# One modulation vector of a decoder trunk summed by ScalarE and an adding transfer instead of VectorE

## The chip, the cores and the metric

One core of one Trainium2 chip. A core has TensorE (PE; its weight loads are listed apart as PEld), VectorE (DVE), ScalarE (ACT), GpSimd (POOL) and SyncE (SP), which run their own instruction queues in order and meet at semaphores, and 16 DMA engines that all queues share. The metric is the device time of one execution in microseconds (us), the median over runs.

## The reference

Two decoder layers on 256 tokens of width 2048, in float32. Each layer is conditioned on one vector c: from it six modulation vectors are computed per layer, each a product of c with a 2048 x 2048 block of `mod_w`.

```
c_act = silu(c)
for layer in range(2):
    mod = c_act @ mod_w[layer] + mod_b[layer]
    sh1, sc1, g1, sh2, sc2, g2 = split(mod, 6)
    h = modulate(rms_norm(x), sh1, sc1)
    y = nsa_mixer(h) if layer == 0 else sb_mixer(h, k_sh, v_sh)
    x = x + g1 * rms_norm(y)
    h = modulate(rms_norm(x), sh2, sc2)
    y = swiglu(h)               # (silu(h @ w_gate) * (h @ w_up)) @ w_out
    x = x + g2 * rms_norm(y)
```

The vector of this case is `g2` of the second layer, the gate of its second mixer (the SwiGLU). It is the last of the 14 vectors and is needed only at the end, when `x + g2 * rms_norm(y)` is formed.

## The kernel before

**Weights.** All matmuls take tiles of 512 x 512 weights, 1 MB each, loaded by SP into a page (128 x 2048 float32) called raw. ScalarE rounds a page into wh (tile type fp32r), VectorE writes the remainder wl = raw - wh, and TensorE then makes three products for each 128 x 128 block of the left side (its high and low halves with wh, its high half with wl), over two halves of the tokens: 24 matmuls of 128 x 512 per tile. The left sides are hhF (the second mixer's normed input) and fa (its activations).

**Pages.** There are 21 pages (`N_PAGES`) for everything of that size: raw, wh, wl, the left sides, modw, macc and others. A page goes from one tenant to the next; the first instruction that writes the new tenant waits, by semaphore, for the last one that used the old.

**The order.** The program is written out in advance by a planner (`Emit`, `pump`, `run`): it keeps estimated clocks of PE, ACT, DVE and the DMA queues and puts each instruction, in the order of these estimates, into its engine's queue. On the chip the order is fixed and only semaphores time it. `fill` puts small idle matmuls (128 x 256, bf16) before a matmul of TensorE where the planner expects TensorE to wait over 1.2 us. Loads are issued by SP in the order of the list `order`; for the last stage `spread` mixes the 16 pages of vector (1, 5) among its weight tiles.

**The vector.** `mac_load` makes the 16 loads of a vector. Page k, called modw, holds rows 128k to 128k + 127 of the block. VectorE forms macc = modw * cact[:, 0] for k = 0, and macc = modw * cact[:, k] + macc for the others (cact is silu(c), one value per partition); then the page is given back. 6 us of the planner's clock after the last page `mod_fin` follows: four matmuls with ones (pmod) sum macc over the partitions, a copy by ScalarE (mrow), transposes, bias and norm weight by VectorE. Later `gate_rows` writes the vector to DRAM and reads it back as the 128 x 2048 tile G, both on GpSimd's queue, which until then carries nothing in this stage. `y_block` multiplies by G.

**The stage.** The second layer's second mixer runs from about 1680 us to the end: six blocks of gate and up products (`ep_gateff` puts silu(gate) into sg, `ep_up` multiplies, transposes on TensorE, aT, and splits into fa), then a first part of the output product (into yp), five more blocks, and the rest of the output product.

Line numbers: in the profile every engine instruction stands at line 118 (119 with the change), the helper that records it; tiles are told apart by name.

Of the kernel before, what the change touches and what calls it, by code (L numbers as in the profile page):

```python
# [12 lines left out]
AF = mybir.ActivationFunctionType  # L13
OP = mybir.AluOpType
# [5 lines left out]
D = 2048  # L20
# [39 lines left out]
FILL_LEAVE = 0.7  # L60
LEADS = (5.0, 5.0, 5.0)
M_FFN = 80

C_ID, C_NTRI, C_ANY, C_NEG1, C_ONE, C_KEEP = 0, 128, 256, 258, 259, 260
C_MASK, C_MASKT, C_CMP, C_COS, C_SIN, C_END = 260, 388, 516, 548, 804, 1060
# [32 lines left out]
class Engine:  # L98
# [5 lines left out]
    def __getattr__(self, op):  # L104
        f = getattr(self.real, op)
        E, eng = self.E, self.name

        def call(*a, **k):
            acc = k.get("accum_out")
            aps = [v for v in list(a) + [v for n, v in k.items() if n != "accum_out"] if hasattr(v, "free_size")]  # L110
            out, ins = aps[0], aps[1:]
            load = 0.0
            if eng == "ACT" and a[2] in TABLES and TABLES[a[2]] != E.table:
                E.table, load = TABLES[a[2]], 1.28
            if eng == "PE":
                E.fill(aps)
            E.enter(eng, _cost(eng, op, out, ins, k, acc), [out] + ([acc] if acc is not None else []), ins, load)
            return f(*a, **k)  # L118

        return call  # L120


def _cost(eng, op, out, ins, k, acc):
    n = out.free_size()
    if eng == "PE":
        if op == "transpose":
            return 0.109
        if ins[1].dtype != F32:
            return max(n / 2400.0 + 0.0133, 0.04)
        if out.shape[0] <= 64 and n >= 128:  # L130
            return n / 2400.0 + 0.09 if out.shape[0] <= 32 else n * 2 / 2400.0 + 0.02
        return 2 * max(n * 2 / 2400.0 + 0.0133, 0.109)
    n = max([n] + [i.free_size() for i in ins])
    if eng == "ACT":
        ptr = sum(hasattr(k.get(x), "free_size") for x in ("bias", "scale")) + (acc is not None)
        return 0.08 + n * 0.000833 + 0.093 * ptr
    if eng == "DMA2":
        return 3.0
    if eng == "DMA":
        return n * 4 * P / 383e3  # L140
    fast = op in ("tensor_scalar", "tensor_copy") and out.space == ins[0].space and list(ins[0].ap)[-1][0] == 1
    ptr = 0.055 * (op in ("tensor_scalar", "scalar_tensor_tensor"))
    return 0.075 + ptr + n / (1920.0 if fast else 960.0)
# [308 lines left out]
def kernel(ctx: ExitStack, tc, consts, x, c, mod_w, mod_b, norm_g, ffn_w_in, ffn_w_out, a_w_in,  # L452
# [8 lines left out]
    E = Emit(nc)  # L461
    V, A, T, DMA = E.V, E.A, E.T, E.D
# [5 lines left out]
    def small(name, n, dt=F32):  # L468
        return cp.tile([P, n], dt, name=name)
# [74 lines left out]
    cact = small("cact", 16)  # L544
# [3 lines left out]
    def modb(vec):  # L548
        l, i = vec
        if l == 2:  # L550
            return vecT[:, 0, 96 + 16 * i:112 + 16 * i]
        return vecT[:, l, 16 * i:16 * i + 16]
# [6 lines left out]
    def mod_src(vec):  # L559
        l, i = vec  # L560
        return (mod_w[l] if l < 2 else kv_mod_w)[:, i * D:(i + 1) * D]
# [9 lines left out]
    macs = {}  # L571

    def mac_load(vec, k):
        st = {}

        def dma():
            st["t"] = E.alloc("pg", "modw")
            DMA.dma_start(st["t"], mod_src(vec)[k * P:(k + 1) * P, :])

        def mac(sl):  # L580
            if k == 0:
                if sl.start == 0:
                    macs[vec] = E.alloc("pg", "macc")
                V.tensor_scalar(macs[vec][:, sl], st["t"][:, sl], cact[:, 0:1], None, op0=OP.mult)
            else:
                V.scalar_tensor_tensor(macs[vec][:, sl], st["t"][:, sl], cact[:, k:k + 1], macs[vec][:, sl],
                                       op0=OP.mult, op1=OP.add)
            if sl.stop == D:
                E.put("pg")
                if k == 15:  # L590
                    E.spawn(after(mod_fin(vec), E.fin + (2.0 if vec[0] == 0 and vec[1] < 5 else 6.0)))

        return Load(("mod", vec, k), "mod", 1 if k == 0 else 0, dma, lambda: E.when(st["t"]),
                    lambda: mac(slice(0, D)))

    def mod_fin(vec):

        yield
        m = macs[vec]
        b = yield from E.get("x", "pmod")  # L600
        for q in range(4):
            T.matmul(b[32 * q:32 * q + 32], ones.to_broadcast([P, 32]), m[:, q * NB:(q + 1) * NB], start=True, stop=True)
        E.put("pg")
        row = yield from E.get("s2", "mrow")
        yield
        A.activation(row, b, AF.Copy)
        yield
        for j in range(4):
            T.transpose(b[:, j * P:(j + 1) * P], row[:, j * P:(j + 1) * P], ident)
        E.put("s2")  # L610
        yield
        v4 = lambda ap: ap.rearrange("p (q j) -> p q j", q=4)
        dst = v4(modT[vec])
        V.tensor_tensor(dst, b.rearrange("p (j q r) -> p q j r", j=4, q=4)[:, :, :, 0], v4(modb(vec)), op=OP.add)
        if vec in gn_of:
            g = vecT[:, 2, 16 * gn_of[vec]:16 * gn_of[vec] + 16] if vec[0] < 2 else vecT[:, 1, 96:112]
            V.scalar_tensor_tensor(dst, dst, 1.0 if vec[0] == 2 or vec[1] in sc_like else 0.0, v4(g),
                                   op0=OP.add, op1=OP.mult)
        E.put("x")
        E.flag(("mod", vec))  # L620
# [489 lines left out]
    def ep_piece(acc, t, place, p, final):  # L1110

        if p:
            yield from E.wait(("part", place, t, p - 1))
        s = yield from part_of(place, t)
        if p == KT - 1 and final[0] == "v":
            yield from ep_v(acc, t, final[1], s, lambda: part_done(place))
            return
        if p == 0:
            A.activation(s, acc, AF.Copy)
        else:  # L1120
            V.tensor_tensor(s, acc, s, op=OP.add)
        E.put("mm")
        E.flag(("part", place, t, p))
        if p == KT - 1:
            yield
            if final[0] == "q":
                yield from ep_q(s, t, final[1], lambda: part_done(place))
            else:
                yield from ep_k(s, t, "ksw", final[1], lambda: part_done(place))
# [378 lines left out]
    for kt in range(KT):  # L1508
        if kt == 0:
            first = [blk[0] for blk in whole]  # L1510
            for seg, nb, place, final in early[:0]:
                first += mm_units(seg, w0, col[seg] + nb * NB, nb, [kt], "hA",
                                  lambda a, t, nb_, place=place, final=final, kt=kt: ep_piece(a, t, place, kt, final))
# [6 lines left out]
        for seg, nb, place, final in early[0 if kt == 0 else 0:]:  # L1520
            emit_plain(mm_units(seg, w0, col[seg] + nb * NB, nb, [kt], "hA",
                                lambda a, t, nb_, place=place, final=final, kt=kt: ep_piece(a, t, place, kt, final)))
# [82 lines left out]
    def mods_of(vecs):  # L1605
        return [("mod", v, k) for v in vecs for k in range(16)]
# [3 lines left out]
    def keys_of(a, b):  # L1610
        ks = []
        for u in units[a:b]:
            k = u.get("key")
            if k and k not in seen:
                seen.add(k)
                ks.append(k)
        return ks
# [4 lines left out]
    def spread(ks, mods, tail, head=0):  # L1622


        tot = sum(cost(k) for k in ks[head:len(ks) - tail])
        o, m, c = [], 0, 0.0
        for i, k in enumerate(ks):
            if i >= head:
                c += cost(k)
            want = min(len(mods), round(len(mods) * c / tot))  # L1630
            while m < want:
                o.append(mods[m])
                m += 1
            o.append(k)
        return o
# [22 lines left out]
    m1 = mods_of([(0, 5), (2, 1), (2, 0), (1, 1), (1, 0)])  # L1658
    order += spread(keys_of(n_l0, n_f0), m1[:M_FFN], TAIL, HEAD)
    order += spread(keys_of(n_f0, n_l1), m1[M_FFN:] + mods_of([(1, 2), (1, 4), (1, 3)]), TAIL, HEAD)  # L1660
    order += spread(keys_of(n_l1, len(units)), mods_of([(1, 5)]), 20, HEAD)

    for k in order:
        if k[0] == "mod":
            E.loads.append(mac_load(k[1], k[2]))
        elif k[0] == "modq" and k[2] == "h":
            E.loads.append(macq_half(k[1], k[3], k[4]))
        elif k[0] == "modq":
            E.loads.append(macq_load(k[1], k[2], k[3]))
        elif k[0] == "w1":  # L1670
            E.loads.append(raw_load(k, a_cmp_w1[0, k[1], k[2] * 1024:(k[2] + 1) * 1024, :]))
        elif k[0] == "wg":
            E.loads.append(w_load(k, w0[:, col["g"]:col["g"] + 3 * H], 16, 3 * H))
        else:
            E.loads.append(w_load(k, wsrc[k]))
# [64 lines left out]
    def after(gen, t, calm=False):  # L1740
        yield t
        while calm and E.urgent:
            yield False
        yield from gen
# [73 lines left out]
```

## Time and profile before

| what | us |
|---|---|
| runs (2) | 2411.55 and 2412.08, median 2411.82 |
| profiled execution, first to last instruction | 2407.8 |
| PE busy | 2356.9 (98%) |
| DVE busy | 1633.4 (68%) |
| ACT busy | 1077.6 (45%) |
| all 16 sums of the vector on VectorE | from 1700.8 to 2232.9 |
| pmod of the vector | 2239.9 |
| gate written by GpSimd, then read back | 2291.7, 2295.2 |

Busy shares are averages over stages; what a change is worth is read in its stage. In a timeline a row gives start, duration, engine, line, operation, tiles and shapes, and in brackets how long the engine had been idle before it and what ended that. In a table by stretches each engine has its busy us and instruction count, then follow the granted TensorE clock (1.00 is full), the share of the DMA engines in use, and GB/s.

### The profile page before, as it was taken

Reading aid. Unit: us, or ns where it says so; the run is one execution under the profiler, and the core shown is the slowest. Engines: PE = TensorE matmul, PEld = TensorE weight load, DVE = VectorE, ACT = ScalarE, POOL = GpSimd, SP = SyncE. Lnnn points to the kernel's source line nnn. Section 1 sums busy time; section 2 is a strip of 40 time slices with the busy share of each in tenths; the row PEclk is TensorE's granted clock in tenths of the full one; section 3 lists DMA queues with packets and bytes.
Section 4 is the critical chain, followed back from the end, with each engine's and each line's share of the span. In section 5 each row is a group of like instructions: output and inputs, shape, how many; then the busy total and the mean of one; then the engine's idle time right before and its main releaser. Section 6 shows DMA issues by size and latency. Waiting matters only on the chain.

```text
span 2407.8 us, 27188 instructions
## 1 busy us (share of the span) xinstructions
PE 2356.9 (98%) x11124; PEld 1906.6 (79%) x11124; DVE 1633.4 (68%) x1346; ACT 1077.6 (45%) x1217; POOL 5.6 (0%) x14
## 2 busy tenths in 40 slices
PE   6999999999999999999999999999999999999998
PEld 4677777877888888888877788887888888888886
DVE  3788789978766667767768778865645454554554
ACT  4343455563433333333455455765433333333342
POOL 0000000000000000000000000000000000000000
PEclk9999999999999999999999999999999999999999
DMA  9998967979887699878758979845756547855642
GB/s 350 389 388 281 354 245 250 362 252 397 283 309 273 224 330 399 327 273 307 260 197 333 339 272 399 315 166 196 269 191 220 200 152 244 304 193 196 221 160 105
DMA packets 265629, 657.54 MB, mean 273 GB/s; under 512 B 12449, under 2 KB 30113, under 8 KB 240161
## 3 DMA queue, kind: packets, MB, share of 16 engines
q1 hardware_dynamic: 263808, 649.13, 75.0%
q0 software_dynamic: 992, 6.32, 0.7%
q8 instruction: 87, 1.43, 0.2%
q10 hardware_dynamic: 704, 0.36, 0.1%
q14 instruction: 38, 0.30, 0.0%
HBM read 653.64 MB, written 2.13 MB: 272 GB/s over the span
## 4 chain that ended last, share of the span: by engine, by line
PE 86%; ACT 4%; DMA 4%; DVE 3%; SPq 1%; issue 1%; ACTq 0%; DVEq 0%
PE acc L118 78%; DMA raw<-in_a_w_in_dram 2%; PE sc L118 1%; SPq L118 1%; DVE wl L118 1%; PE oT L118 1%; PE z L118 1%; ACT wh L118 1%; ACT hf L118 1%; ACT junk L118 1%; PE aT L118 1%; DMA modw<-in_mod_w_dram 1%; PE pmod L118 1%; DMA modq<-in_mod_w_dram 1%; PE hT L118 1%
## 5 line engine op out<-in xcount | busy, mean ns | idle before, releaser
L118 DVE TENSOR_TENSOR wl<-raw,wh 128x2048 fp32r<-128x2048 f32 (+2 forms) x392 | 880.0, 2249 | 516.9 <-ACT wh L118 477.8
L118 ACT ACTIVATE wh<-raw 128x2048 fp32r<-128x2048 f32 (+2 forms) x392 | 734.6, 1880 | 683.5 <-PE acc L118 478.7
L118 PE MATMUL acc<-wh,hhF 128*128 128x512 f32 x2816 | 883.7, 392 | 0.0
L118 PEld LDWEIGHTS acc<-wh,hhF 128*128 128x128 f32 x2816 | 530.4, 188 | 113.7 <-issue 4.2
L118 PE MATMUL acc<-wl,hhF 128*128 128x512 f32 x1408 | 549.3, 390 | 0.0
L118 DVE SCALAR_TENSOR_TENSOR macc<-modw,cact,macc 128x2048 f32<-128x2048 f32 x180 | 422.5, 2347 | 38.1 <-DMA modw<-in_mod_w_dram 29.2
L118 PE MATMUL acc<-wh,fa 128*128 128x512 f32 x1408 | 437.4, 390 | 0.0
L118 PEld LDWEIGHTS acc<-wh,fa 128*128 128x128 f32 x1408 | 264.3, 188 | 55.8 <-issue 0.8
L118 PEld LDWEIGHTS acc<-wl,hhF 128*128 128x128 f32 x1408 | 265.4, 188 | 53.8
L118 PE MATMUL acc<-wl,fa 128*128 128x512 f32 x704 | 273.9, 389 | 0.0
L118 PE MATMUL acc<-wh,hA 128*128 128x512 f32 x640 | 220.7, 404 | 1.4 <-DVE hA L118 0.7
L118 PE MATMUL acc<-wh,hhK 128*128 128x512 f32 x512 | 161.4, 392 | 0.9 <-ACT wh L118 0.7
L118 PEld LDWEIGHTS acc<-wl,fa 128*128 128x128 f32 x704 | 132.2, 188 | 26.9
L118 PEld LDWEIGHTS acc<-wh,hA 128*128 128x128 f32 x640 | 120.1, 188 | 39.7 <-issue 15.0
L118 PE MATMUL acc<-wl,hA 128*128 128x512 f32 x320 | 125.4, 392 | 3.0 <-DVE wl L118 3.0
L118 PEld LDWEIGHTS acc<-wh,hhK 128*128 128x128 f32 x512 | 96.0, 188 | 22.6 <-ACT wh L118 1.1
L118 PE MATMUL acc<-wl,hhK 128*128 128x512 f32 x256 | 100.3, 392 | 1.2 <-DVE wl L118 1.2
L118 ACT ACTIVATE fa<-aT 128x512 fp32r<-128x512 f32 x44 | 26.0, 594 | 162.8 <-PE aT L118 150.6
L118 PE MATMUL acc<-wh,hhB 128*128 128x512 f32 x256 | 87.5, 401 | 0.0
L118 PE MATMUL acc<-wh,oA 128*128 128x512 f32 x256 | 84.8, 398 | 0.0
L118 PE MATMUL acc<-wh,oB 128*128 128x512 f32 x256 | 82.4, 394 | 0.0
L118 PEld LDWEIGHTS acc<-wl,hA 128*128 128x128 f32 x320 | 60.4, 189 | 13.6 <-DVE wl L118 4.2
(183 smaller groups left out, 1664.9 us busy)
## 6 DMA issues: line engine op xcount, KB each, us to landing
raw<-in_ffn_w_in_dram SPq DMA_DIRECT2D x176, 1024.0 KB, 5.3
modw<-in_mod_w_dram SPq DMA_DIRECT2D x160, 1024.0 KB, 7.1
raw<-in_ffn_w_out_dram SPq DMA_DIRECT2D x88, 1024.0 KB, 5.3
raw<-in_a_w_in_dram SPq DMA_DIRECT2D x40, 1024.0 KB, 14.2
modq<-in_mod_w_dram SPq DMA_DIRECT2D x32, 1024.0 KB, 14.1
modw<-in_kv_mod_w_dram SPq DMA_DIRECT2D x32, 1024.0 KB, 5.7
raw<-in_kv_w_dram SPq DMA_DIRECT2D x32, 1024.0 KB, 7.6
raw<-in_a_w_out_dram SPq DMA_DIRECT2D x16, 1024.0 KB, 7.1
```

What stands on the lines that cost most here:

```text
L118: return f(*a, **k)
```

## The change

For vector (1, 5) alone, ScalarE multiplies page k in place by cact[:, k] (k = 0 directly into macc), and a DMA begun by GpSimd with `accum_op=add` adds the page onto macc in SBUF. The page is given back when the planner expects that transfer to have landed; the planner's cost of it is 6.0 in place of 3.0, to which it adds 2.5 of latency. The loads of the vector now wait for ScalarE's turn in `pump` (`eng="ACT"`), and `mod_fin` follows 2 us after the last transfer's estimated landing.

```
+BY_DMA = ((1, 5),)
...
     if eng == "DMA2":
-        return 3.0
+        return 6.0 if n == D and k.get("accum_op") else 3.0
...
+        def scale_add():
+            if k == 0:
+                macs[vec] = E.alloc("pg", "macc")
+                A.activation(macs[vec], st["t"], AF.Copy, scale=cact[:, 0:1])
+            else:
+                A.activation(st["t"], st["t"], AF.Copy, scale=cact[:, k:k + 1])
+                E.D2.dma_start(macs[vec], st["t"], accum_op=OP.add)
+            E.put("pg")
+            if k == 15:
+                E.spawn(after(mod_fin(vec), E.fin + 2.0))
+
+        if vec in BY_DMA:
+            return Load(("mod", vec, k), "mod", 1 if k == 0 else 0, dma, lambda: E.when(st["t"]), scale_add, eng="ACT")
```

Ahead of the second layer's second mixer no engine's order changes, and SP's list of loads is the same to the end. VectorE has 16 instructions fewer, ScalarE 16 more, GpSimd 15 transfers more. Two places matter here. Rows give operation, output and inputs with their buffer numbers, size, and the semaphores that are waited for: DMASW are those of GpSimd's transfers, DMAHW of SP's loads.

ScalarE in the output product's first part, before: five rows in a row, each wh taking a page that VectorE or TensorE hands back.

```order
L118 ACTIVATE wh_13598<-raw_13435 128x2048 [waits DMAHW2_49,PE_49]
L118 ACTIVATE wh_13629<-raw_13465 128x2048 [waits DMAHW3_49,DVE_49,PE_49]
L118 ACTIVATE wh_13661<-raw_13495 128x2048 [waits DMAHW4_49,DVE_49,PE_49]
L118 ACTIVATE wh_13691<-raw_13617 128x2048 [waits DMAHW6_49,DVE_49,PE_49]
L118 ACTIVATE yp_13531<-acc_13540 128x512 [waits PE_49]
```

With the change, the same place:

```order
L119 ACTIVATE wh_13619<-raw_13456 128x2048 [waits DMAHW2_49,PE_49]
L119 ACTIVATE modw_13608<-modw_13608,cact 128x2048 [waits DMAHW5_49,DVE_49]
L119 ACTIVATE wh_13651<-raw_13486 128x2048 [waits DMAHW3_49,PE_49]
L119 ACTIVATE wh_13681<-raw_13516 128x2048 [waits DMAHW4_49,DMASW7_49,Activation_49]
L119 ACTIVATE wh_13713<-raw_13638 128x2048 [waits DMAHW6_49,DVE_49,PE_49]
```

The scaling of page modw_13608 (the ninth of the vector, k = 8) stands between two wh; the second wh behind it is the next tenant of that page and waits for DMASW7, which the transfer macc<-modw_13608 counts up.

TensorE at the second of the four weight tiles of a gate block, before: the tile's first wh matmul is followed at once by its wl matmul (hhF are the left sides).

```order
L118 MATMUL acc_13097<-wh_13038,hhF_1779_11605 128x512
L118 MATMUL acc_13097<-wl_13039,hhF_1779_11605 128x512
L118 MATMUL acc_13097<-wh_13038,hhF_1779_11605 128x512
L118 MATMUL acc_13078<-wh_13072,hhF_1781_11615 128x512 [waits Activation_49]
L118 MATMUL acc_13078<-wl_13073,hhF_1781_11615 128x512
```

With the change:

```order
L119 MATMUL acc_13086<-wh_13114,hhF_1781_11615 128x512 [waits Activation_49]
L119 LDWEIGHTS identb
L119 MATMUL idle_13131<-identb 128x256
L119 LDWEIGHTS identb
L119 MATMUL idle_13131<-identb 128x256
```

13 idle matmuls now stand between the tile's first wh and first wl matmul, the only ones that the change adds. On ScalarE the split of this tile (wh_13114, before wh_13072) has moved behind the scaling of page modw_13017 and two fa; its wl takes the page that the transfer of modw_13017 frees.

## The prediction

> **What bounds the kernel now.** I read the page first, then the table by stretches over the last second-mixer stage, where the vector is summed, then the timelines of ScalarE, VectorE and the load queue there.
>
> ```profile
> span 2407.8 us, 27188 instructions
> PE 2356.9 (98%) x11124; PEld 1906.6 (79%) x11124; DVE 1633.4 (68%) x1346; ACT 1077.6 (45%) x1217; POOL 5.6 (0%) x14
> ...
> core 0: us, PE busy (x) PEld busy (x) DVE busy (x) ACT busy (x) POOL busy (x), PEclk, DMA share, GB/s
> ...
> 1860.00:1960.00 100.00, 100.00 (x451) 82.77 (x450) 49.68 (x28) 38.58 (x26) 0.00 (x0) 1.00 0.57 196
> 1960.00:2060.00 100.00, 100.00 (x443) 82.81 (x442) 49.23 (x22) 37.88 (x24) 0.00 (x0) 1.00 0.64 222
> 2060.00:2160.00 100.00, 100.00 (x449) 82.80 (x448) 52.62 (x28) 40.28 (x28) 0.00 (x0) 1.00 0.70 242
> ```
>
> TensorE (PE) is busy for all 100 us of each stretch at full clock, VectorE (DVE) half, ScalarE (ACT) 40%. So nothing that only shortens VectorE's work can shorten this stage; a change can cost here, by making TensorE wait. What it waits for first is the split of the next weight tile, which runs just in time:
>
> ```profile
> 1984.14 1.92 ACT L118 ACTIVATE wh<-raw 128x2048 fp32r<-128x2048 f32 x1 [3.52 <-PE acc L118]
> 1989.58 1.92 ACT L118 ACTIVATE wh<-raw 128x2048 fp32r<-128x2048 f32 x1 [3.52 <-PE acc L118]
> ...
> 1982.86 2.35 DVE L118 SCALAR_TENSOR_TENSOR macc<-modw,cact,macc 128x2048 f32<-128x2048 f32 x1
> ...
> 1991.53 2.29 DVE L118 TENSOR_TENSOR wl<-raw,wh 128x2048 fp32r<-128x2048 f32 x1 [3.14 <-ACT wh L118]
> ...
> 1994.82 0.62 PE L118 MATMUL acc<-wh,fa 128*128 128x512 f32 x2
> 1995.28 0.39 PE L118 MATMUL acc<-wl,fa 128*128 128x512 f32 x1
> ```
>
> A tile's wh begins when TensorE hands back a page (`<-PE acc`), every 5.44 us; its wl ends at 1991.53 + 2.29 = 1993.82. The release at 1995.0 marks the tile's start on TensorE, so its first wl matmul is the one at 1995.28. Spare time: 1995.28 - 1993.82 = **1.46 us**.
>
> **The change, part by part.** VectorE loses 15 sums and one product, ScalarE gains 16 scalings:
>
> ```profile
> L118 DVE SCALAR_TENSOR_TENSOR macc<-modw,cact,macc 128x2048 f32<-128x2048 f32 x180 | 422.5, 2347 | 38.1 <-DMA modw<-in_mod_w_dram 29.2 <-DMA modw<-in_kv_mod_w_dram 8.2
> L118 DVE TENSOR_SCALAR macc<-modw,cact 128x2048 f32<-128x2048 f32 x12 | 15.4, 1283 | 3.8 <-DMA modw<-in_mod_w_dram 1.7 <-PE acc L118 1.2 <-PE pmod L118 0.9
> ```
>
> That is 15 x 2.35 + 1.28 = 36.5 us off VectorE and, at the wh row's 1.92 us, 16 x 1.92 = 30.7 us onto ScalarE. Neither is on the path: TensorE covers both. A scaling fits in the 3.52 us that ScalarE idles before each wh. The load queue's order does not change at all.
>
> What is new on the path is the page. Before, a modw page was free when VectorE's sum ended. Now it is free when the transfer that adds it has landed, and the next user of that page waits for it, in order, on its own engine, with everything queued behind it. I call T the time from the scaling's end to that landing. Of the fifteen pages, four go to a load next, whose tile is split several tiles later; three to a wl, one to an fa and seven to a wh on ScalarE, the first or second behind the scaling. Of these wh, four stand where the split runs just in time: behind the pages modw_13285, modw_13608 (shown above), modw_13826 and modw_14592. When these pages were loaded before, how long modw took to land in this stage, and when the wh in question ran:
>
> ```profile
> 1922.18 0.34 SPq L118 DMA_DIRECT2D modw<-in_mod_w_dram  x1
> 1977.53 0.34 SPq L118 DMA_DIRECT2D modw<-in_mod_w_dram  x1
> 2015.61 0.34 SPq L118 DMA_DIRECT2D modw<-in_mod_w_dram  x1
> 2141.68 0.34 SPq L118 DMA_DIRECT2D modw<-in_mod_w_dram  x1
> ...
> DMA to landing us min/median/max: 4.7/4.9/8.8
> ...
> 1934.23 1.92 ACT L118 ACTIVATE wh<-raw 128x2048 fp32r<-128x2048 f32 x1 [3.52 <-PE acc L118]
> 2027.66 1.92 ACT L118 ACTIVATE wh<-raw 128x2048 fp32r<-128x2048 f32 x1 [3.52 <-PE acc L118]
> 2154.22 1.91 ACT L118 ACTIVATE wh<-raw 128x2048 fp32r<-128x2048 f32 x1
> ```
>
> The page issued at 1977.53 lands at 1982.4 and is scaled by 1984.4; the wh ran at 1989.58, so T may be 5.2 us, and 6.7 with the spare 1.46. Likewise 1929.0 to 1934.23 and 2022.4 to 2027.66: 5.2 and 6.7 each; 2148.5 to 2154.22: 5.7 and 7.2. Every us of T beyond that is a us of TensorE, four times.
>
> T has no row. The nearest are the 1 MB gate rows that GpSimd's queue already carries (first line), and how busy the DMA engines are where the four transfers fall (the column before the last):
>
> ```profile
> DMA to landing us min/median/max: 4.5/4.8/5.9
> ...
> 1929.00:1937.00 8.00, 8.00 (x39) 6.60 (x39) 4.57 (x4) 3.62 (x2) 0.00 (x0) 1.00 1.00 344
> 1984.00:1993.00 9.00, 9.00 (x41) 7.46 (x40) 4.97 (x3) 3.84 (x2) 0.00 (x0) 1.00 0.97 332
> 2022.00:2031.00 9.00, 9.00 (x41) 7.45 (x40) 4.96 (x3) 4.22 (x3) 0.00 (x0) 1.00 0.96 319
> 2148.00:2157.00 9.00, 9.00 (x44) 7.45 (x43) 3.58 (x4) 2.40 (x2) 0.00 (x0) 1.00 0.83 273
> ```
>
> Below: adding costs nothing, T is 4.5 plus some 0.5 of handing over, 5. Above: reading the page, reading the sum and writing it follow one another, each at the slowest 5.9: 18. I take two passes, since an add must read twice what a copy reads: 9.6, with the handing over **T = 10**; that the engines are already 83 to 100% busy with weights keeps me from going lower. The weights share the engines the other way too, but a tile loaded at 1982.97 is split at 1995.02 and landed in 5:
>
> ```profile
> 1982.97 11.25 SPq L118 DMA_DIRECT2D raw<-in_ffn_w_out_dram  x4
> ...
> 1995.02 1.92 ACT L118 ACTIVATE wh<-raw 128x2048 fp32r<-128x2048 f32 x1 [3.52 <-PE acc L118]
> ...
> raw<-in_ffn_w_out_dram SPq DMA_DIRECT2D x33, 1024.0 KB, 5.2
> ```
>
> That is 7 us of cover, and I count nothing; if a load came later than that, its lateness would be one more term. The four waits are then 3.3 + 3.3 + 3.3 + 2.8 = **12.7 us**.
>
> The Trainium skill bears on that price twice. Its page "Collectives: The Full Stack" (The bandwidth ceiling: the fold count and why AG ≠ RS ≠ AR) says that a reduce is slower than a copy for its second source read, not for the arithmetic; no run shows it yet. With the 2.0 us + bytes/436e3 of "DMA: Bandwidth & Descriptors" (Anatomy of one DMA — SWDGE), two reads of 1 MB make an estimated T of 6.8, and the sum below would be about 3.
>
> A wait that long also costs clock. TensorE's idle time before a row, and the granted clock after it:
>
> ```profile
> 1675.61 2.76 PE L118 MATMUL xT<-K,xn 128*128 128x128 f32 x16 [2.13 <-DVE xn L118]
> ...
> 1676.60:1680.00 3.40, 3.40 (x14) 3.01 (x13) 1.91 (x5) 2.44 (x8) 0.00 (x0) 0.50 0.00 0
> ...
> 87.11 0.50 PE L118 MATMUL acc<-wl,hA 128*128 128x512 f32 x1 [1.82 <-DVE wl L118]
> ...
> 85.00:90.00 5.00, 3.18 (x16) 2.14 (x19) 4.89 (x6) 3.10 (x4) 0.00 (x0) 1.00 1.05 386
> ```
>
> After a gap of 2.13 us the clock was 0.50 for 3.4 us, 1.7 us lost; after 1.82 it stayed 1.00. All four waits are over 2.13: 4 x 1.7 = **6.8 us**. "TensorE: Matmul & The Clock Gate" of the Trainium skill (Part 1: The HAM clock gate) puts the drop after an idle window of about 3.4 us; by that this term would be nothing and the sum 6.8 lower. The row above disagrees, and decides.
>
> One more place, where the order itself has moved: ScalarE now takes the scaling of modw_13017 and both fa ahead of the wh that ran at 1889.01.
>
> ```profile
> 1879.10 0.34 SPq L118 DMA_DIRECT2D modw<-in_mod_w_dram  x1
> ...
> 2225.19 0.34 SPq L118 DMA_DIRECT2D modw<-in_mod_w_dram  x1
> ...
> 1889.01 1.92 ACT L118 ACTIVATE wh<-raw 128x2048 fp32r<-128x2048 f32 x1 [5.84 <-DVE macc L118]
> ...
> 1895.64 0.60 ACT L118 ACTIVATE fa<-aT 128x512 fp32r<-128x512 f32 x1 [1.70 <-PE aT L118]
> 1896.14 1.91 ACT L118 ACTIVATE wh<-raw 128x2048 fp32r<-128x2048 f32 x1
> ...
> L118 PE MATMUL pmod<-macc,K x16: 592/604/616, 1610.5 to 2239.9; 128*32 128x512 f32 x16
> ```
>
> The second fa's transposes come six matmuls (0.227 us each, 5.44 over 24), 1.4 us, earlier, so that fa starts at 1894.3, the wh half a us behind it as in the last two ACTIVATE rows, and wl ends at 1894.8 + 1.92 + 2.29 = 1899.0. TensorE wants it one matmul after the tile's start at 1896.14, at 1896.4: **2.6 us**. The 13 new idle matmuls stand inside that gap; they do not add to it, and they keep the clock up. The wl's page is the one scaled by 1885.9, and with T = 10 it is back in time.
>
> The sum's own end is in time too. The last page, issued at 2225.19, is scaled by 2232.0, so it is summed at 2242; pmod, the matmul that reads the sum, ran at 2239.9 and is 18 matmuls, 4.1 us, later in the new order. It would wait from T = 12 on.
>
> Sum: 12.7 + 6.8 + 2.6 = 22.1 us on the profiled 2407.8. The runs' median, 2411.8, lies 4.0 above that span; I add to it: **2434 us**, 0.9% slower, inside the 2% that a measurement of this kernel can tell from no change.
>
> **The rivals.** *One pass.* The add rides on the copy, T is 5 to 6.7: the four pages come in time, only the 2.6 us of order are left, 2414. For it: GpSimd's 1 MB took 4.5 to 5.9; against it: engines 83 to 100% busy at those places.
>
> *Slow adding.* The passes follow one another, or adding has a slower rate of its own, and T is 18. Then the four wait 11.3 three times and 10.8, the moved wl 1885.9 + 18 - 1896.7 = 7.2 on top of its 2.6, pmod 6, with six half-clock windows: 44.7 + 9.8 + 6 + 10.2 = 71 us, 2483, slower by 2.9%. It passes 2% at T = 14.3. For it: no row shows an adding transfer, and weights and add share the engines. Against it: no row suggests a rate below that of a copy.
>
> *Hidden gain.* VectorE's 36.5 us come back as time. That needs TensorE waiting for VectorE here, and the stretches show 100.00 of 100.00 busy: 2412 at best, no change.
>
> **How the numbers follow.** Late pages, T 7 to 14.3: 0.55, with 2415 to 2460. One pass: 0.24. Slow adding: 0.18. Hidden gain: 0.03, of which 0.01 beyond 2%. So faster 0.01, same 0.81, slower 0.18. The range goes from 2411, below the one-pass case, to 2466, where T is 15.2; what is left out is the rest of slow adding.
>
> **What would show it.** The adding transfers' issue to landing on GpSimd's queue, near 10 us; ScalarE's wh waiting for a DMA of macc or modw four times, 3 us late each; TensorE gaps of about 3 us near 1943, 2001, 2043 and 2174, followed by clock 0.50; 13 idle matmuls near 1896; VectorE some 36 us less busy, ScalarE 31 more. Wrong if the transfers land in under 6.7 us, if loads behind them become the wait, or if the stages before 1690 us change at all, since no instruction is moved there.

## The result, and the profile after

The changed kernel took 2442.16 us (two runs, 2439.71 and 2444.61) against 2411.82 before: a ratio of 1.0129, 95% interval 1.0105 to 1.0153. It is slower by 1.3%, where 0.9% was forecast. The profiled execution spans 2442.8 us, 35.0 more than that of before, where the prediction's sum was 22.1; by the medians of the runs the growth is 30.3.

The page of the changed kernel, and of its groups the two that the change touches (busy us and mean ns of one, then the idle time before it):

```profile
span 2442.8 us, 27279 instructions
...
PE 2370.5 (97%) x11137; PEld 1914.1 (78%) x11137; DVE 1597.7 (65%) x1330; ACT 1108.0 (45%) x1233; POOL 18.6 (1%) x29
...
L119 DVE SCALAR_TENSOR_TENSOR macc<-modw,cact,macc 128x2048 f32<-128x2048 f32 x165 | 387.2, 2347 | 30.5 <-DMA modw<-in_mod_w_dram 20.5 <-DMA modw<-in_kv_mod_w_dram 9.5
...
L119 ACT ACTIVATE modw<-modw,cact 128x2048 f32<-128x2048 f32 x15 | 30.1, 2008 | 39.4 <-DMA modw<-in_mod_w_dram 39.4
```

VectorE is busy 35.7 us less and ScalarE 30.4 more, as worked out, and neither bought anything. The stage shows what it cost; the same kind of stretches as before:

```profile
core 0: us, PE busy (x) PEld busy (x) DVE busy (x) ACT busy (x) POOL busy (x), PEclk, DMA share, GB/s
1860.00:1960.00 100.00, 95.55 (x428) 78.00 (x427) 43.02 (x25) 38.67 (x26) 1.70 (x2) 0.98 0.68 216
1960.00:2060.00 100.00, 94.81 (x402) 77.15 (x401) 37.29 (x17) 39.23 (x25) 1.72 (x2) 0.97 0.64 201
2060.00:2160.00 100.00, 96.66 (x423) 79.36 (x422) 43.90 (x23) 44.23 (x30) 2.58 (x3) 0.98 0.87 277
2160.00:2260.00 100.00, 95.28 (x418) 78.12 (x417) 41.59 (x24) 38.34 (x26) 1.72 (x2) 0.97 0.66 209
```

TensorE, busy 100.00 us of 100 before, now idles 3 to 5 of them, and its clock is no longer 1.00. Its waits in the whole stage, with their sum, number and longest, name the splits and once the second half of silu(gate) x up, and that stands behind a late wl on VectorE:

```profile
PE acc L119 <- DVE wl L119: 9.9, 6, 1.8
PE acc L119 <- ACT wh L119: 6.7, 5, 3.2
PE aT L119 <- DVE sg L119: 3.0, 1, 3.0
```

How long the transfers took, by the list of DMA issues, and the spread of their landings:

```profile
macc<-modw POOLq DMA_DIRECT2D x15, 1024.0 KB, 10.8
...
DMA to landing us min/median/max: 7.5/10.8/12.8
```

And how one of them holds ScalarE. The rows are ScalarE's own timeline at k = 7; in brackets is how long it had idled:

```profile
1929.11 1.92 ACT L119 ACTIVATE wh<-raw 128x2048 fp32r<-128x2048 f32 x1 [3.52 <-PE acc L119]
1934.00 2.01 ACT L119 ACTIVATE modw<-modw,cact 128x2048 f32<-128x2048 f32 x1 [2.98 <-DMA modw<-in_mod_w_dram]
1935.92 1.90 ACT L119 ACTIVATE wh<-raw 128x2048 fp32r<-128x2048 f32 x1
1944.34 1.92 ACT L119 ACTIVATE wh<-raw 128x2048 fp32r<-128x2048 f32 x1 [6.53 <-issue]
```

The scaling ends at 1936.01, the transfer lands at 1943.9 by its last packet, and the wh that takes the page starts at 1944.34 where the rhythm of 5.44 us would have had it at 1940.0. (The releaser is named "issue" here; at k = 13 the same wait is put down to the transfer, 6.77 us of it.) The wait was forecast for this place and this instruction.

Setting the starts of TensorE's 9216 acc matmuls against those of before, number by number, gives the growth place by place, gap and half-clock window together (each place from one level stretch of the shift to the next):

| place | forecast us | measured us |
|---|---|---|
| head of the program, no instruction moved | 0 | 2.3 |
| moved order near 1896 | 2.6 | 3.5 |
| page k = 7 (1946) | 5.0 | 4.7 |
| page k = 8 (2006) | 5.0 | 4.7 |
| page k = 9 (2049) | 5.0 | 4.6 |
| load of page 11 (2102) | 0 | 5.4 |
| page k = 13 (2186) | 4.5 | 7.4 |
| page k = 15 and pmod (2276) | 0 | 2.5 |
| sum, before rounding | 22.1 | 35.0 |

The 2.3 us of the head come from places whose code is the same in both kernels (half-clock windows near 90 and 257 us and a wait that differs from one execution to the next). The six kernels below that have this code unedited too (copy, other next user, page 11 later, both together, the two with traffic) stand between 1.6 us ahead of the kernel before and 2.2 behind it at 1680 us, and the changed kernel's other run spans 2437.9. So this term is chance and not the change.

### The profile page after: what moved, and what is told of

Same layout as the page of the kernel before. It is cut to its first block, busy times and chain, and to the rows that moved or that the text cites. A ratio compares the mean times of both kernels' runs of the same rounds, so it can differ in the third digit from the quotient of the medians.

```text
span 2442.8 us, 27279 instructions
## 1 busy us (share of the span) xinstructions
PE 2370.5 (97%) x11137; PEld 1914.1 (78%) x11137; DVE 1597.7 (65%) x1330; ACT 1108.0 (45%) x1233; POOL 18.6 (1%) x29
## 3 DMA queue, kind: packets, MB, share of 16 engines
HBM read 653.64 MB, written 2.13 MB: 268 GB/s over the span
## 5 line engine op out<-in xcount | busy, mean ns | idle before, releaser
L119 DVE SCALAR_TENSOR_TENSOR macc<-modw,cact,macc 128x2048 f32<-128x2048 f32 x165 | 387.2, 2347 | 30.5 <-DMA modw<-in_mod_w_dram 20.5
```

## The experiments

The theory is that of the prediction: a page is late by what the adding transfer takes beyond the spare time, its next user holds an in-order engine, and the gap halves TensorE's clock besides. Its rivals are traffic (the transfers delay the weights) and ScalarE (30 us more on the engine whose wh run just in time). The experiments with a profile also have the time of the stage alone, from one and the same acc matmul (the 6301st, near 1727) to the last one: 672.1 us before, 704.8 with the change.

**A copy in place of the sum.**

```
-                E.D2.dma_start(macs[vec], st["t"], accum_op=OP.add)
+                E.D2.dma_start(macs[vec], st["t"])
```

> The 15 transfers copy the scaled page over macc instead of adding it, so the running sum is left out of the computation; every engine's order and every page stay as in the change. Late pages: an adding packet took 628 ns and a copying one of the same 8 KB took 309, 8 packets lie on each DMA engine, so each landing comes 2.5 us earlier. The page waits behind k = 7, 8, 9, 13 and 15 (2.9, 2.5, 2.7, 4.7, 1.8 us of TensorE gap) shrink to 0.4, 0, 0.2, 2.2 and 0, the place behind k = 11 from 3.3 to 0.8, half-clock windows are left after k = 13 alone (some 2), and the moved order near 1896 still costs 3.2: about 9 above the kernel before, 2421. If the weights' loads suffer from the traffic, half of the traffic goes and so half of the loss: 2427. If ScalarE's scalings and their place in its order cost the time, nothing changes: 2442.

Measured: 2424.09 us, ratio 1.0059 (1.0044 to 1.0074); the stage 684.0. First the rows of the list of DMA queues and issues of the copying kernel (packets, MB, share of 16 engines between 1684 and 2300), then its waits of TensorE:

```profile
q0 software_dynamic: 2160, 15.73, 6.6%
...
macc<-modw POOLq DMA_DIRECT2D x15, 1024.0 KB, 6.4
```

```profile
PE acc L119 <- DVE wl L119: 4.5, 4, 1.8
PE acc L119 <- ACT wh L119: 2.1, 3, 1.4
```

For the adding kernel the queue's row in that window is

```profile
q0 software_dynamic: 2160, 15.73, 12.9%
```

The same packets and bytes take the engines twice the time when they add, which is what two passes would take, as the prediction chose. With landings 4.4 us earlier in the median (6.4 us against 10.8 from the issue), 20.8 of the stage's 32.7 us are gone, no engine's order having changed. ScalarE as the cause is out: it does the same work in the same order. The engines' time of these transfers has halved too, so this run alone does not tell a late page from traffic; the next one does. The 3 us above the expectation lie at page 11 (two gaps of 2.1 us together where 0.8 was expected) and at k = 13 (3.3 where 2.2 was), whose transfer still took 10.2.

**Another next user for the page.**

```
+    scr = nc.dram_tensor("scr", (1, D), F32, kind="Internal").ap()
...
                 E.D2.dma_start(macs[vec], st["t"], accum_op=OP.add)
+                E.D2.real.dma_start(scr, st["t"][0:1])
```

> Behind each adding transfer GpSimd sends one more, 8 KB of the scaled page to DRAM. It is nearly nothing as traffic, but the page then goes to another next user: those of k = 7, 8, 9, 13 and 15 go to a load of weights instead of a wh, that of k = 10 to a wh far behind instead of a load; the order of the instructions on every engine is that of the change. Late pages: the five wh no longer wait, SP's wait that held up the load of page 11 is gone, and SP's new waits are covered by the 12 us and more that a loaded tile lies before its split. Only the moved order near 1896 is left, 3.2 us: 2415, at most 2420. If it is traffic, or ScalarE's scalings in its order, the time stays near 2442.

Measured: 2423.94 us, 1.0054 (1.0039 to 1.0069); the stage 684.8. The adding transfers are as slow as ever, and where the changed kernel had its first three waits TensorE now never waits (one stretch of the table by stretches, then the transfers):

```profile
1940.00:2060.00 120.00, 120.00 (x533) 99.42 (x532) 52.20 (x25) 51.70 (x33) 4.17 (x6) 1.00 0.71 236
```

```profile
macc<-modw POOLq DMA_DIRECT2D x15, 1024.0 KB, 10.9
```

This is the cleanest of the runs: same orders, same adding transfers, the same traffic but for 15 transfers of 8 KB (13.0% of the engines' time against 12.9%), only the tenants differ, and 20 us of the stage go. SP does wait for the pages instead (48.2 us in seven waits, 37.5 in five with the change), but its loads are covered. Two parts of the expectation failed, and with them its number, at most 2420: the place of page 11 stayed, and k = 14 showed a new gap of 1.6. At page 11:

```profile
2083.92 2.01 ACT L119 ACTIVATE modw<-modw,cact 128x2048 f32<-128x2048 f32 x1 [9.60 <-DMA modw<-in_mod_w_dram]
2085.83 3.69 ACT L119 ACTIVATE wh<-raw 128x2048 fp32r<-128x2048 f32 x2
```

ScalarE stands 9.6 us for the load of page 11 with two wh behind it, without SP being held there as long as in the changed kernel: it waits 4.3 us, for a split, ahead of this load, against 10.6 for a page (below).

**Page 11's scaling behind the two wh.**

```
-... lambda: E.when(st["t"]), scale_add, eng="ACT")
+... lambda: E.when(st["t"]) + (8.0 if k == 11 else 0.0), scale_add, eng="ACT")
```

> The planner is told that page 11 is ready 8 us later, so that its scaling stands behind the next two wh on ScalarE instead of ahead of them; nothing else moves, but the page's next user is then a load and not a wl. In the change SP waits 10.5 us for the transfer of page 10 before it can issue a load, page 11 is loaded behind that, and ScalarE holds two wh behind the scaling until it has landed. If that chain costs the 3.3 us gap near 2102 and the half-clock window behind it, 5 to 5.5 us go: 2437. If another wait takes its place there (the tiles' own loads, that SP's wait made late), 2442.

Measured: 2438.83 us, 1.0123 (1.0106 to 1.0140), 3.3 less by the medians; the stage 697.6, 7.2 less. By the starts of the acc matmuls 5.2 of the 7.2 lie at page 11; k = 8 costs 2.1 less, where the last gap of 1.8 us is this time not followed by half clock, and k = 13 1.2 more. At the place of page 11 nothing is left of gap or clock:

```profile
2085.00:2110.00 25.00, 25.00 (x112) 20.71 (x111) 11.09 (x5) 11.93 (x8) 0.86 (x1) 1.00 0.97 324
```

So it is the scaling's place in ScalarE's queue that costs there: an instruction that waits for a load with two wh behind it. In the changed kernel its load was late because SP stood for page 10's transfer (10.6 us, by the waits of the load queue between 2080 and 2087 us) and then sent four loads in a row:

```profile
SPq L119 <- DMA macc<-modw: 10.6, 1, 10.6
```

```profile
2088.44 0.51 SPq L119 DMA_DIRECT2D modw<-in_mod_w_dram  x1
...
2099.59 2.01 ACT L119 ACTIVATE modw<-modw,cact 128x2048 f32<-128x2048 f32 x1 [11.53 <-DMA modw<-in_mod_w_dram]
2101.51 3.69 ACT L119 ACTIVATE wh<-raw 128x2048 fp32r<-128x2048 f32 x2
```

**Both together.** The edits of the last two kernels in one.

> The kernel with the other next users, and in it the scaling of page 11 behind the two wh instead of ahead of them. There ScalarE idled 9.6 us for that page's load, TensorE had two gaps of 1.8 us and a half-clock window of 6.8 us, together some 7 us. By late pages and held-up wh nothing is left but the moved order near 1896, and the time is 2424 - 7 = 2417. If the tiles behind that place are late for another reason (the loads themselves), 2424.

Measured: 2419.91 us, 1.0035 (1.0022 to 1.0049); the stage 679.9. The gaps at page 11 are gone; 4.9 of the 7 us are had. What is left of the change, 7.8 us in the stage, is by the starts of the acc matmuls the moved order (3.9), 0.7 near page 11, 2.1 where page 12's transfer, 12 us long, is waited for (a gap of 1.8), and 1.1 at k = 14 (a gap of 0.9). The late pages move on to the next user that is short of time.

**The clock alone.** 105 idle matmuls at five places, the waits untouched:

```
+KEEP = {(("p1", 0, 0), 1, "end"): 20, (("p1", 1, 5), 0, "wh"): 4, (("p1", 1, 5), 0, "wl"): 13, ...}
...
+            T.real.matmul(o[:, 0:2 * P], zerob, E.filler[1], start=False, stop=False, skip_group_check=True)
```

> The change, with 105 idle matmuls (zero weights, added to the sum that is being formed) ahead of the waiting matmuls behind k = 7, 8, 9, 11 and 13, a little fewer than fill the gaps that were seen. All waits stay. If a window of half clock follows each gap and costs time of its own, those windows go: 1.4 + 1.7 + 1.7 + 1.6 + 2.4 = 8.8 us less, 2433. If the half clock lies under the waits and costs nothing, 2442, or a little more where the idle matmuls overrun a gap.

Measured: 2435.42 us, 1.0102 (1.0086 to 1.0119), and 7.6 us less in the stage (697.3). Three places of the changed kernel, and the same three with the idle matmuls:

```profile
1945.00:1955.00 10.00, 7.01 (x28) 5.55 (x27) 6.47 (x5) 4.14 (x4) 0.00 (x0) 0.83 0.44 161
2005.00:2015.00 10.00, 7.47 (x25) 5.48 (x24) 4.49 (x2) 3.67 (x3) 0.00 (x0) 0.83 0.90 317
2047.00:2057.00 10.00, 7.34 (x26) 5.40 (x25) 4.57 (x2) 4.68 (x4) 0.00 (x0) 0.83 0.86 311
```

```profile
1940.00:1950.00 10.00, 9.38 (x54) 7.55 (x53) 4.50 (x4) 4.81 (x4) 0.00 (x0) 1.00 0.69 226
2000.00:2010.00 10.00, 9.61 (x52) 7.51 (x51) 4.49 (x2) 4.31 (x3) 0.00 (x0) 1.00 0.92 332
2040.00:2050.00 10.00, 8.97 (x46) 6.87 (x45) 4.58 (x2) 4.69 (x4) 0.00 (x0) 1.00 0.86 308
```

A mean of 0.83 over 10 us is one window of 3.4 us at half clock, 1.7 us lost; with the idle matmuls it is 1.00. At page 11 and k = 13 it goes from 0.83 and 0.72 to 1.00 as well. The clock is a price of its own, 7.6 of the 8.8 us that were expected.

**Traffic alone.** The kernel before, with the running sum sent to DRAM twice behind each sum:

```
+    scr = nc.dram_tensor("scr", (2, P, D), F32, kind="Internal").ap()
...
+                if vec == (1, 5) and k < 15:
+                    for i in range(2):
+                        E.D2.real.dma_start(scr[i], macs[vec])
```

> The kernel before, VectorE's sums and order included; behind each of its first 15 sums GpSimd sends the running sum to DRAM twice, 1 MB each time, so that each of the 16 DMA engines carries 16 more packets of 8 KB, some 5 us, as the adding transfer's 8 packets of 628 ns are. No page is held up by it: only the next sum, 26 us and more later, waits for it. Late pages: the weights' loads have their cover of 7 us and more, so the time stays that of the kernel before, 2410 to 2413. If the traffic is what costs the time, by late loads, it is 2425 or more.

Measured: 2425.62 us, 1.0059 (1.0045 to 1.0072). The number fits the rival, the reason doesn't: one wait made most of it, of VectorE for the extra transfer itself.

```profile
1713.53 2.35 DVE L118 SCALAR_TENSOR_TENSOR macc<-modw,cact,macc 128x2048 f32<-128x2048 f32 x1 [13.05 <-DMA scr<-macc]
```

The second sum was due right behind the first, not 26 us later as the expectation had it. The same without the first pair of transfers (`0 < k < 15`):

> As the last kernel with added traffic, but without the two transfers behind the first sum: there VectorE's second sum, due at once, waited 13 us for them, TensorE stood 9.2 us, and that wait is the experiment's own and not the change's. What was left beside it was one gap of 1.5 us near 2092, where VectorE waited 8.7 us for the load of page 11. Late pages: 2411 to 2414, that gap and at most a half-clock window. If the traffic makes the weights late throughout, 2420 or more, with gaps spread over the stage.

Measured: 2414.07 us, 1.0011 (1.0002 to 1.0021); the stage 674.4, 2.3 more than before. In it TensorE waits once, and VectorE's wait for the load of page 11 is twice that of before, 4.72 us there:

```profile
PE acc L118 <- DVE wl L118: 2.0, 1, 2.0
```

```profile
2082.02 2.35 DVE L118 SCALAR_TENSOR_TENSOR macc<-modw,cact,macc 128x2048 f32<-128x2048 f32 x1 [9.20 <-DMA modw<-in_mod_w_dram]
```

GpSimd's queue takes 11.7% of the engines' time between 1684 and 2300 us here, near the 12.9% of the adding transfers, though it writes to DRAM and not to SBUF. So traffic of this size costs 2 to 3 us, all at the one load that is sent in a burst; it landed 11.7 us after its issue, 7.3 before. The rest of the weights have their cover.

**VectorE adds.** ScalarE scales as in the change, VectorE adds the page:

```
-                E.D2.dma_start(macs[vec], st["t"], accum_op=OP.add)
+                V.tensor_tensor(macs[vec], macs[vec], st["t"], op=OP.add)
```

> ScalarE scales every page in place as in the change, and VectorE adds it onto macc (tensor_tensor, some 2.3 us) in place of the transfer. The scalings stand on ScalarE as in the change, but near 1896 the wh is again ahead of the second fa; pages come back when VectorE is done. Late pages: no transfer, no wait; what may be left is the scaling of page 11 ahead of two wh, at most 5 us: 2411 to 2416. If 30 us more on ScalarE, whose wh run just in time, are what costs the time, it stays near 2440.

Measured: 2411.31 us, 1.0003 (0.9994 to 1.0013). ScalarE's 30 us more cost nothing once the page comes back with VectorE. Page 11's scaling is ahead of two wh here too and costs nothing that can be measured; that no transfer makes its load late is the likely reason, and no run separates it. Of this kernel only the time is used.

**The clock in the kernel before.** The kernel before has such windows too.

```
+    def still(b):
+        for _ in range(17):
+            T.real.matmul(b[:, 0:2 * P], *E.filler, start=True, stop=True)
```

> The kernel before, with 17 idle matmuls written ahead of the transposes at three places where TensorE waits some 2.2 us for VectorE (near 513, 595 and 1674 us), into the bank that the transposes then overwrite; no wait is moved. If over half of a 3.4 us window of idle time halves the clock of the next window, each filled gap saves up to 1.7 us where the window fell so, 3 to 5 us in all: 2406 to 2408. If the clock follows something else, or the matmuls overrun the gaps, no gain: 2410.5 or more.

Measured: 2409.39 us, ratio 0.9990 (0.9982 to 0.9999): 0.1% below the kernel before, with an interval that ends just under 1, and less than expected. Its three places, of which the kernel before showed each at 0.83:

```profile
512.00:522.00 10.00, 9.56 (x59) 7.66 (x58) 7.12 (x16) 6.27 (x17) 0.00 (x0) 1.00 0.52 203
594.00:604.00 10.00, 9.66 (x54) 7.79 (x53) 7.83 (x5) 1.36 (x2) 0.00 (x0) 1.00 1.05 406
1672.00:1682.00 10.00, 9.55 (x58) 7.35 (x56) 6.96 (x16) 7.51 (x20) 0.00 (x0) 1.00 0.32 105
```

The windows are gone. That 1.2 us are had and not 3 to 5 has three reasons that the traces suggest and no run separates. A window costs less here than 1.7 us: by the starts of the acc matmuls the first two places gain 2.5 us together and the third 0.8. In other executions a gap of 2.2 us falls across two windows and is followed by no half clock anyway (the profile of the kernel with other next users has none near 516 and 598, and gains 2.4 there without any idle matmul). And the wait near 257 differs by itself between executions (5.43 us in this profile, 3.96 in that of before).

## Why the prediction came out, point by point

**PE bounds the stage, the work moved is worth nothing.** Right: 36 us off VectorE, 30 onto ScalarE, no gain; and with VectorE adding, 1.0003.

**T.** Right in its mean. From the scaling's end to the last packet the fifteen transfers took 7.5 to 12.8 us, 10.2 in the mean, against the 10 chosen. The doubled packet time agrees with a second pass, but a rate of adding half that of copying would look the same, and no run separates them. How the 10 was put together came out less well: one pass, in the copying kernel, took 6.8 in the mean and not 4.8 + 0.5, and adding put 3.4 on top and not 4.8, so that the two errors cancel. What the sum did not have is the spread: the four pages that it priced had 7.9, 9.0, 9.3 and 12.0.

**Four waits of 3.3, 3.3, 3.3 and 2.8.** Right in place and in the limit; the sum, 12.9 against 12.7, is luck. The gaps were 3.0, 2.5, 2.7 and 4.7 (at k = 13 3.19 and 1.53). T less the gap is the limit up to which a page costs nothing: 6.5, 6.6 and 7.3 at k = 8, 9 and 13, where 6.7, 6.7 and 7.2 were worked out. Only at k = 7 it was 4.9, since the page's load landed later in ScalarE's rhythm than before: the scaling ended 1.5 us behind the point where a wh was due, and made that wh late too. So T under 10 made the waits at k = 8 and 9 smaller than forecast, and the 12.0 of k = 13 made up for it.

**Pages counted as harmless.** Here the sum failed. "Of the fifteen pages, four go to a load next, whose tile is split several tiles later": the tile of page 10's load was indeed not late, but SP's queue behind that load was, and in it the load of page 11, and behind that load's scaling two wh: 5.4 us. This is the term for a late load that the prediction named and put at nothing. The prediction asked what is queued behind the waiting instruction for ScalarE and not for SP. And the wh behind page 15 was not counted among the tight ones, but was: a gap of 1.8 and 2.5 us in all.

**Clock, 4 x 1.7.** Right in price, wrong in the rule. Half of the time that TensorE was busy in the half-clock windows is 1.4, 1.7, 1.4 and 2.3 us at the four places, 6.9 together against 6.8, and 1.6 at page 11. The rule "a gap over 2.13 us" does not hold: at k = 8 the longest gap was 1.83. The last section has what does.

**The moved order, 2.6.** 3.5 measured. The 13 idle matmuls stood inside the gap as said. The first wh ran at 1897.08, which less the head's 2.3 is the 1894.8 that was worked out. Of the 0.9 us more, 0.7 are the page's, which "with T = 10 is back in time": T was 10.9 there, and the wl, whose wh was done at 1899.0, began only at 1899.66, behind the landing at 1899.27 (VectorE's timeline).

```profile
1899.66 4.50 DVE L119 TENSOR_TENSOR wl<-raw,wh 128x2048 fp32r<-128x2048 f32 x2 [1.75 <-DMA macc<-modw]
```

**pmod.** It waited as little as said: T at the last page was 8.3.

**Loads, 0.** 2.3 us with nearly the same amount of traffic and no waits on pages: the load of page 11 again.

The Trainium skill's figure for such a transfer ("DMA: Bandwidth & Descriptors", Anatomy of one DMA — SWDGE), by which T was an estimated 6.8, is below each of the fifteen: nearest is 7.5, at k = 12, where SP had issued one load in the 6 us before. Its rule in "Collectives: The Full Stack" (The bandwidth ceiling: the fold count and why AG ≠ RS ≠ AR), that the second source read is what makes a reduce dearer, agrees with the queue's share, 12.9% against 6.6%, which shows twice the time and not what it is spent on.

**Its signs of being wrong.** The transfers did not land in under 6.7 us. The stages before 1690 us did change, by the 2.3 us of the head, which other kernels with the same code there show as well. And one load behind the transfers did become the wait, that of page 11.

Of the rivals, one pass is out by the copying kernel, slow adding by T itself, and the hidden gain by the change itself, which took 35.7 us off VectorE and gave no time back. So the forecast of 2434 was right in its mechanism and 8 us low; what was left out are the two places of page 11 and page 15 (7.9 us), and the longer transfer at k = 13 (2.9).

## What to carry to other kernels

Handing work to a transfer also hands it the buffer: price the time until the buffer is back, for its next user and for everything queued behind that user, on the load queue as much as on the engines. An engine with idle time in the mean is no reason to move work off another one when neither is the bound. Where a tensor engine's waits can't be taken away, matmuls that keep its clock up can pay: here 105 of them took 7.6 us off a stage of 704.8.

## What the runs showed of the hardware

**The clock's window stands on a fixed grid.** Every half-clock window of the changed kernel begins a whole number of 3.413 us after the others, and the clock of a window follows how idle TensorE was in the window before. Three pairs of neighbours from the table by stretches, idle share in the first and clock in the second:

```profile
1945.20:1948.62 3.42, 1.04 (x5) 0.54 (x3) 2.33 (x2) 1.06 (x1) 0.00 (x0) 1.00 1.05 401
1948.62:1952.03 3.41, 2.80 (x9) 2.41 (x10) 2.18 (x3) 2.89 (x3) 0.00 (x0) 0.50 0.10 35
2006.64:2010.05 3.41, 1.58 (x7) 1.18 (x7) 3.41 (x2) 1.43 (x1) 0.00 (x0) 1.00 0.72 241
2010.05:2013.47 3.42, 3.42 (x10) 2.67 (x9) 0.74 (x1) 0.60 (x1) 0.00 (x0) 0.50 0.98 346
2276.30:2279.71 3.41, 1.99 (x14) 0.87 (x14) 3.41 (x3) 0.83 (x1) 0.00 (x0) 1.00 0.73 235
2279.71:2283.12 3.41, 3.41 (x20) 2.69 (x17) 2.30 (x5) 1.09 (x2) 0.00 (x0) 1.00 1.02 360
```

With 2.38 and 1.83 us idle of 3.41 the next window is at 0.50, with 1.42 it is not, and a gap of 1.82 that falls across two windows passes. One window near 254 us with 1.83 us idle was not followed by half clock either, so the limit lies about there. The ten profiles of this case other than that of the kernel in which VectorE adds say the same: between 60 and 2390 us no window at full clock with up to 1.73 us idle was followed by half clock, every one with 2.1 or more was, and between them both occur. "TensorE: Matmul & The Clock Gate" of the Trainium skill (Part 1: The HAM clock gate) says that the window is 3413 ns and runs freely; the trace agrees. It says that one idle window halves the clock; here about half a window of idle time is enough.

**The wait before the first packet.** In the changed kernel it took from GpSimd's issue to the first packet of an adding transfer 1.4 to 2.3 us where SP had issued one load in the 6 us before (k = 3, 7, 8, 9, 12, 15), 4.3 to 5.1 where it had issued two or more (k = 1, 2, 4, 10, 13), and 2.8 to 5.0 where one had been issued and the next followed within half a us (k = 5, 6, 11, 14); from the first packet to the end of the last it was always 5.7 to 7.8. The wait is most of what makes T 7.5 in one place and 12.8 in another (1.4 and 5.1 us of it). That SP's loads cause it was not tested; in the copying kernel k = 5 had one load before it and one right behind as well, and waited 1.1.

**Who gets a page.** The planner's own figure for the time at which a page is free does not decide its next user: with one more small transfer that reads the page, which the planner does not see, five pages went to a load instead of a wh although no engine's order changed; in the traces SP waits for pages seven times instead of five.
